# Pairing heads in the second mixer's attention: scores in the two row halves, values in the two column halves of the array

## The chip, the cores and the metric

The kernel runs on one core of a Trainium2 chip. The metric is the device time of one execution in microseconds: 2069.24 us is the median of three timed runs before the change (2062.05, 2069.24, 2071.39).

TensorE (PE) multiplies, PEld is its weight loader, VectorE is DVE, ScalarE is ACT, GpSimd is POOL, and SyncE (SP) issues the DMAs that carry weights from memory.

## What is computed

Two transformer blocks in a row on 256 tokens of width 1024, all in float32. Each block has a token mixer and then a mixture of experts. The change touches the attention of the second block's mixer alone:

```python
o_a = neighbourhood_attention(q_a * scale, k_a, v_a, k_ca, v_ca, rpb)   # 8 heads, each with its own keys
qb = axial_rope(rmsnorm(q_b, g_qn), row, col) * scale
kb = axial_rope(rmsnorm(k_b, g_kn), row, col)
k_all = concatenate([kb, k_cb]);  v_all = concatenate([v_b, v_cb])      # 256 tokens and 256 context rows
o_b = blocked_gqa(qb, k_all, v_all)                                     # 8 heads in 2 groups of 4
y = (sigmoid(g_a) * (o_a @ w_out_a) + sigmoid(g_b) * (o_b @ w_out_b)) @ w_o
```

A head has 64 dimensions. Each head attends from 256 queries to 256 tokens (in the neighbourhood attention with a bias and a window) and to 256 rows of context, so a softmax row has 512 entries. In the grouped attention heads 0 to 3 share the keys and values of group 0, heads 4 to 7 those of group 1. Behind the mixer the router picks 4 of 32 experts for each token, and the experts' weights follow.

## The kernel before

The kernel fixes the order of PE, DVE and ACT by hand: each of these engines runs its instructions in the order in which the source emits them. Weights come through a ring of 2 MB slots (`Ring`, from L98); SP issues the load of the next piece when a slot is given back, at L132.

The attention is a software pipeline over 32 steps (`Step`, from L2085, and the loop that ends at L2207). A step is one head and one half of the queries (128 rows). The first 16 steps are the neighbourhood heads, the last 16 the grouped heads. Head `h = 2b + s` in both halves; in the loop the query half `n` runs fastest, then `s`, then the pair number `b`. A step has these parts:

- `scores` (L2099): two products of 64 rows x 128 queries with 64 x 256 keys, tokens and context, into one of two `sc` buffers in PSUM. The queries and keys of a head lie in 64 of the 128 partitions, so a product uses one row half of the array (`tile_position=(p0, 0)`).
- `largest` (L2105 and L2106 grouped, L2109 to L2112 neighbourhood, DVE): the row maximum, with the bias added for the neighbourhood heads.
- `exps` (L2118, or L2120 and L2121, ACT): exponentials and their row sums into the tile `e`.
- `scaled` (L2126 to L2128, DVE): division by the sum.
- `turned` and `copied` (L2133 on PE, L2137 on ACT): four 128 x 128 transposes and a copy to `eT`, of which there are two buffers.
- `values` (L2145, PE): four products of 128 rows x 64 columns with `eT`, into 64 of the 128 partitions of the single tile `o` (one column half of the array). After the last step of a pair of heads ACT casts `o` out (L2148), and DVE makes the rest of the cast (`ended`, L2153).

An iteration emits the scores of step i, the values of step i - 2, the scaling of step i - 1, the maximum of step i, the exponentials of step i, and the transposes of step i - 1. Between them stand two calls `feed(2)`, which emit other projections (L703 on PE, with their casts L715 on ACT and L716 on DVE; each weight is split into a high and a low part), and three calls of `next(feed.behind)`, which sum condition vectors (L1949 ACT, L1951 POOL, L1952 and L1954 DVE, L479 PE) until they are done, late in the neighbourhood half. At step 16 `heads_to_columns` (L2166 to L2172) transposes the keys and queries of the grouped heads. A float32 product appears in the trace as two records.

The first mixer has a similar attention (loop at L1339). Its `values(pair)` (L1324) emits two heads in turn, each in its column half; its scores (L1280, L1281) are emitted one head at a time.

Behind the loop follow `w_out_a`, `w_out_b` and `w_o` (again L703), the router, and the second mixture of experts, whose weight loads (`w_gu`, `w_dn`) need the experts' order from the router and start with `ring.open()`.

Of the kernel before, what the change touches and what calls it, by code (L numbers as in the profile page):

```python
# [12 lines left out]
F32 = mybir.dt.float32  # L13
# [4 lines left out]
ALU = mybir.AluOpType  # L18
# [3 lines left out]
P = 128  # L22
D = 1024
T = 256
# [133 lines left out]
def _body(tc, nc, a, off, es, stop, dump):  # L158
    V, S, G, PE = nc.vector, nc.scalar, nc.gpsimd, nc.tensor
# [4 lines left out]
    def ps(tag, bufs, name=None):  # L164
        return psum.tile([P, 512], F32, tag=tag, bufs=bufs, name=name or tag)
# [77 lines left out]
    for q in range(8):  # L243
# [4 lines left out]
        for e in (4 * q, 4 * q + 2):  # L248
            pieces.append((("dn1", e), lambda t, e=e: load_dn1(t, e)))
    seq = [(key, piece_cols(win2, c0, n)) for key, c0, n in (("ka", 0, 512), ("qa", 1280, 512), ("kvb", 1024, 256), ("va", 512, 512),  # L250
           ("qb", 1792, 512), (("gab", 0), 2304, 512), (("gab", 1), 2816, 512), (("gab", 2), 3328, 512), (("gab", 3), 3840, 512))]
    for nm in ("w_out_a_2", "w_out_b_2"):
        seq.append((nm, lambda t, nm=nm: [(t.rearrange("p (c f) -> p c f", c=4), a[nm][0].rearrange("(c p) f -> p c f", p=P))]))
    for piece, conds in zip(seq, CONDS):
        pieces.append(piece)
        for i in conds:
# [726 lines left out]
    class Scan:  # L983
# [45 lines left out]
        def ended(self):  # L1029
            yb = yT[:, self.b]  # L1030
            V.scalar_tensor_tensor(yb, uT[:, self.b], dcol[:, self.b:self.b + 1], Scan.py[:, :T], op0=ALU.mult, op1=ALU.add)
            gelu(yb, yb, 5, yT[:, self.b + 1] if self.b < 3 else last_rot[:, 0, 0])
# [232 lines left out]
    class Look:  # L1265
# [10 lines left out]
        def scores(self):  # L1276
            self.pt = pt = ps("sc", 2)
            r = slice(64 * self.s, 64 * self.s + 64)
            q, kk = qT[r, self.blk], kz[r, self.br, self.gp]
            PE.matmul(pt[:, :P], q[:, :P], kk[:, :P], start=True, stop=True, tile_position=(64 * self.s, 0))  # L1280
            PE.matmul(pt[:, P:P + T], q[:, P:], kk, start=True, stop=True, tile_position=(64 * self.s, 0))  # L1281
# [803 lines left out]
    class Step:  # L2085
        def __init__(self, grouped, b, s, n):
            self.grouped, self.b, self.s, self.n = grouped, b, s, n
            self.h = 2 * b + s
            self.last = s == n == 1

        def scores(self):
            self.pt = pt = ps("sc", 2)
            if self.grouped:
                g, i = divmod(self.h, 4)
                p0, lq, keys = 64 * g, qbT[64 * g:64 * g + 64, i, :], (kbT, kbc)
            else:
                p0, lq, keys = 64 * self.s, qaT[64 * self.s:64 * self.s + 64, self.b, :], (kaT[:, self.b, :], kac[:, self.b, :])
            for i, kk in enumerate(keys):
                PE.matmul(pt[:, T * i:T * i + T], lq[:, P * self.n:P * self.n + P], kk[p0:p0 + 64], start=True, stop=True, tile_position=(p0, 0))  # L2099

        def largest(self):
            self.e = paw.tile([P, 512], F32, tag="e", bufs=3, name="e")
# [33 lines left out]
            self.eT = paw.tile([P, 512], F32, tag="eT", name="eT")  # L2136
            S.copy(self.eT, self.pt2)  # L2137

        def values(self):
            if (self.s, self.n) == (0, 0):  # L2140
                Step.po = ps("o", 1)
            out = Step.po[64 * self.s:64 * self.s + 64, P * self.n:P * self.n + P]
            v, vc, c0 = (vb, vbc, 64 * (self.h // 4)) if self.grouped else (va, vac, 64 * self.h)
            for j in range(4):
                PE.matmul(out, (v if j < 2 else vc)[:, j % 2, c0:c0 + 64], self.eT[:, P * j:P * j + P], start=(j == 0), stop=(j == 3),  # L2145
                          tile_position=(0, 64 * self.s))
            if self.last:
                S.copy(*self.ends(0))  # L2148

        def ended(self):  # L2150
            if self.last:
                hi, src = self.ends(0)
                V.tensor_tensor(self.ends(1)[0], src, hi.bitcast(F32), op=ALU.subtract)  # L2153

        def ends(self, i):

            dst, po = (obT if self.grouped else oaT)[i][:, self.b, :], Step.po[:, :T]
            if self.grouped:
                return dst, po
            return dst.rearrange("p (n t) -> p n t", n=2), backwards(po.rearrange("p (n t) -> p n t", n=2))  # L2160

    def heads_to_columns():

# [12 lines left out]
        V.tensor_scalar(x1[:, n], x1[:, n], rr[:, n, 3:4], None, op0=ALU.mult)  # L2176
    feed(64)
    feed.next = 1 << 30
    steps = [Step(grouped, b, s, n) for grouped in range(2) for b in range(4) for s in range(2) for n in range(2)]
    prev = last = None  # L2180
    for i, st in enumerate(steps + [None, None]):
        if i == 16:
            heads_to_columns()
            sg[1] = pk.tile([P, 4, T], F32, tag="sg2", name="sg2")
        if i == 18:
            obT.extend(pcx.tile([P, 4, T], F32R, tag=t, name="obT" + x) for t, x in (("kac", "h"), ("vac", "l")))
        if st:
            st.scores()
        if last:
            last.values()  # L2190
        if prev:
            prev.scaled()
        if st:
            st.largest()
        if last:
            last.ended()
        next(feed.behind, None)
        feed(2)
        if st:
            st.exps()  # L2200
        next(feed.behind, None)
        if prev:
            prev.turned()
            prev.copied()
        feed(2)
        next(feed.behind, None)
        prev, last = st, prev  # L2207
    if stop == "att2":
        nc.sync.dma_start(dump["oaT"], oaT[0].bitcast(F32))
        nc.sync.dma_start(dump["obT"], obT[0].bitcast(F32))  # L2210
# [631 lines left out]
```

## Time and profile before

| | before |
|---|---|
| median of 3 runs | 2069.24 us |
| profiled execution, its own time | 2064.46 us |
| its span | 2062.7 us |
| PE busy | 1801.3 us, 87% |
| DVE busy | 851.9 us, 41% |
| ACT busy | 547.0 us, 27% |
| DMA, mean | 306 GB/s |

The page cuts the span into 40 slices of 51.6 us; a digit is the busy share in tenths, and PEclk the granted clock of TensorE in tenths of full speed. The attention lies in slices 17 to 20 (counted from 1).

```profile
PE   5898998989898888999989689986799988999865
DVE  6998888453213237775554112221031211212112
PEclk7998899899999998799988989999899999999986
DMA  8634337866799976551346999999999999899996
```

A mean over the span mixes stages with different limits, so the change has to be read in the window of its own stage, and what follows has to be read for whether it starts earlier when the stage ends earlier.

### The profile page before, as it was taken

To read this page: it belongs to the slowest core of one execution; us is meant where nothing else is said; L and a number is where in the kernel's file an instruction comes from. 1 tells how busy PE (TensorE), PEld (TensorE's weight loads), DVE (VectorE), ACT (ScalarE), POOL (GpSimd) and SP (SyncE) were. 2 spreads that over 40 slices of the span, in tenths; PEclk is the share of its full clock that TensorE was granted. 3 is DMA by queue.
4 is the path that set the end of the run, shared out by engine and by line. 5 is a ranking of instruction groups with operands and counts; after the bars stand their busy time and mean duration, and the time that the engine had idled before them with its cause. 6 is when DMAs were issued, how large, how long until landed. Compare 5 with 4: busy or idle time off the path is not lost. (4 is left out here: it accounts for less than half of the span.)

```text
span 2062.7 us, 25525 instructions
## 1 busy us (share of the span) xinstructions
PE 1801.3 (87%) x10043; PEld 1015.8 (49%) x10043; DVE 851.9 (41%) x1832; ACT 547.0 (27%) x1184; POOL 258.7 (13%) x232
## 2 busy tenths in 40 slices
PE   5898998989898888999989689986799988999865
PEld 3677777876554437788964223332233333333211
DVE  6998888453213237775554112221031211212112
ACT  4443566232011125555432002110011111112001
POOL 2576322110000004430020000000000000000000
PEclk7998899899999998799988989999899999999986
DMA  8634337866799976551346999999999999899996
GB/s 259 229 113 163 111 107 228 276 246 248 287 364 397 393 282 200 194 184 59 128 166 269 423 416 424 420 423 423 417 419 419 424 420 420 340 421 419 423 422 256
DMA packets 172650, 630.82 MB, mean 306 GB/s; under 512 B 25408, under 2 KB 32000, under 8 KB 152032
## 3 DMA queue, kind: packets, MB, share of 16 engines
q1 hardware_dynamic: 172096, 628.04, 78.2%
q8 instruction: 89, 1.46, 0.3%
q10 hardware_dynamic: 288, 0.52, 0.1%
q0 software_dynamic: 128, 0.39, 0.1%
q14 instruction: 49, 0.40, 0.1%
HBM read 627.88 MB, written 1.05 MB: 305 GB/s over the span
## 5 line engine op out<-in xcount | busy, mean ns | idle before, releaser
L2543 PE MATMUL mm<-w,xT 128*64 128x512 f32 x1472 | 330.7, 603 | 0.0
L2543 PEld LDWEIGHTS mm<-w,xT 128*64 128x64 f32 x1472 | 103.2, 139 | 204.2 <-issue 198.6
L2634 PE MATMUL o<-w,aT 128*64 128x512 f32 x640 | 152.4, 612 | 3.2 <-DMA w<-in_w_dn 3.2
L2577 PE MATMUL mm<-w,xT 128*32 128x512 f32 x768 | 102.6, 663 | 39.1 <-DMA w<-in_w_gu 39.1
L2552 DVE TENSOR_SCALAR g<-mm 128x512 f32<-128x512 f32 x23 | 15.9, 692 | 261.2 <-PE mm L2543 261.2
L2811 POOL TENSOR_TENSOR fin<-acc,fin 128x512 f32<-128x512 f32 x1 | 1.3, 1275 | 975.4 <-DVE acc L2809 975.4
L716 DVE TENSOR_TENSOR lo<-w,hi 128x512 fp32r<-128x512 f32 x126 | 100.0, 806 | 30.4 <-ACT hi L715 28.4
L703 PE MATMUL mm<-hTh,scratch 128*128 128x256 f32 x392 | 98.0, 317 | 11.7 <-DVE scratch L716 11.7
L715 ACT CAST hi<-w 128x512 fp32r<-128x512 f32 x126 | 76.6, 618 | 63.7 <-PE mm L703 55.2
L2609 PE MATMUL o<-w,aT 128*32 128x512 f32 x384 | 70.8, 781 | 25.3 <-DMA w<-in_w_dn 23.3
L2634 PEld LDWEIGHTS o<-w,aT 128*64 128x64 f32 x640 | 45.4, 140 | 89.5 <-issue 81.8
L2554 ACT ACTIVATE s<-g 128x512 f32<-128x512 f32 x23 | 14.5, 632 | 274.5 <-DVE g L2552 274.4
L703 PEld LDWEIGHTS mm<-hTh,scratch 128*128 128x128 f32 x392 | 71.4, 203 | 29.9 <-issue 14.8
L1655 PE MATMUL mm<-w,xT 128*32 128x512 f32 x640 | 73.6, 605 | 7.2 <-DVEq L1841 2.7
L2649 DVE SCALAR_TENSOR_TENSOR yl<-yy,wc,yh 128x512 fp32r<-128x512 f32 (+1 forms) x30 | 21.4, 749 | 137.1 <-ACT yh L2648 136.9
L2577 PEld LDWEIGHTS mm<-w,xT 128*32 128x32 f32 x768 | 22.7, 114 | 105.4 <-DMA w<-in_w_gu 60.9
L703 PE MATMUL mm<-hT3h,lo 128*128 128x256 f32 x192 | 61.1, 318 | 9.0 <-DVE lo L716 6.4
L2639 ACT COPY yy<-o 64x512 f32<-64x512 f32 x40 | 23.2, 580 | 159.8 <-PE o L2634 159.5
L1630 PEld LDWEIGHTS sc<-Sm,x 128*128 128x128 f32 x256 | 61.7, 335 | 6.6 <-issue 5.0
L2664 DVE TENSOR_TENSOR acc<-acc,sc 128x512 f32<-128x512 f32 x56 | 37.0, 685 | 66.7 <-PE sc L2656 66.7
L1630 PE MATMUL sc<-Sm,x 128*128 128x128 f32 x256 | 63.2, 411 | 1.3 <-DVE Sm L1621 1.2
L703 PE MATMUL mm<-scratch 128*128 128x256 f32 x216 | 63.8, 295 | 0.0
(706 smaller groups left out, 3593.0 us busy)
## 6 DMA issues: line engine op xcount, KB each, us to landing
w<-in_w_gu SPq DMA_DIRECT2D x128, 2048.0 KB, 19.8
w<-in_w_dn SPq DMA_DIRECT2D x63, 2048.0 KB, 22.9
w<-in_w_in SPq DMA_DIRECT2D x20, 2048.0 KB, 10.5
w<-in_moe_w_gate SPq DMA_DIRECT2D x32, 1024.0 KB, 10.6
w<-in_moe_w_up SPq DMA_DIRECT2D x32, 1024.0 KB, 12.8
w<-in_moe_w_down SPq DMA_DIRECT2D x32, 1024.0 KB, 13.8
w<-in_ada_w SPq DMA_DIRECT2D x12, 2048.0 KB, 9.6
w<-in_w_mod SPq DMA_DIRECT2D x12, 2048.0 KB, 9.1
```

Source lines behind the costliest of these rows:

```text
L703: PE.matmul(out, x, y, start=start and i == 0, stop=stop and i == 2)
L715: S.copy(hi, src)
L716: return parts, lambda: V.tensor_tensor(lo, src, hi.bitcast(F32), op=ALU.subtract)
L1630: PE.matmul(pt[:, P * cc:P * cc + P], xv1[:, n, c, :], Sm[:, n].rearrange("p e s -> p (e s)"), start=(n == 0), stop=(n == 1))
L1655: PE.matmul(pg[32 * j:32 * j + 32, :].rearrange("p (j f) -> p j f", j=2), xT[:, c, 32 * j:32 * j + 32], w[:, c % 2], start=(c == 0), stop= ...
L2543: PE.matmul(pg[i][64 * j:64 * j + 64, :], bcast(ident[:, q:q + 1], [P, 64]) if c < 0 else xT[:, c, :], bgu if c < 0 else w[:, o:o + 512], ...
L2577: PE.matmul(pg[32 * t:32 * t + 32, :], xT[:, c, :], w[:, 512 * ij:512 * ij + 512], start=False, stop=(c == 7), tile_position=(0, 32 * t))
L2609: PE.matmul(pd[32 * t:32 * t + 32, :], aT[:, f % 4, 2 * (1 - e) + f // 4, :], w[:, 512 * j:512 * j + 512], start=False, stop=(f == 7), til ...
L2634: PE.matmul(pd[64 * j:64 * j + 64, :], aT[:, f % 4, f // 4, :], w[:, 512 * j:512 * j + 512], start=False, stop=(f == 7), tile_position=(0, ...
L2639: S.copy(y[:, 512 * j:512 * j + 512], pd[64 * j:64 * j + 64, :])
L2649: V.scalar_tensor_tensor(yl[:, o], y[:, o], back[1], yh[:, o].bitcast(F32), op0=ALU.mult, op1=ALU.subtract)
L2664: V.tensor_tensor(o, o, pc, op=ALU.add)
```

## The change

Two heads now go together, `s = 0` and `s = 1` of the same pair `b` and the same query half `n`; the loop's order is pair, query half, head. `scores(pair)` emits the four products of the two heads in turn, one in the row half 0 to 63 and one in the row half 64 to 127, each head into its own `sc` buffer. It is emitted for the next pair at the end of every odd iteration, and for the first pair ahead of the loop. `values(pair)` emits the eight products of two heads in turn, one in each column half, at every odd iteration for the steps i - 3 and i - 2. All else of a step stays one head at a time. The loop has 35 iterations instead of 34, and `heads_to_columns` stands in iteration 15 instead of 16.

So that two grouped heads lie in different row halves, the grouped pair `b` is now the heads `b` and `4 + b`, one of each group, instead of `2b` and `2b + 1`. The rows of `w_out_b` are loaded in the matching order, in two DMAs of 64 partitions each instead of one of 128.

```diff
-    for nm in ("w_out_a_2", "w_out_b_2"):
-        seq.append((nm, lambda t, nm=nm: [(t.rearrange("p (c f) -> p c f", c=4), a[nm][0].rearrange("(c p) f -> p c f", p=P))]))
+    seq.append(("w_out_a_2", lambda t: [(t.rearrange("p (c f) -> p c f", c=4), a["w_out_a_2"][0].rearrange("(c p) f -> p c f", p=P))]))
+    seq.append(("w_out_b_2", lambda t: [(t.rearrange("p (c f) -> p c f", c=4)[64 * g:64 * g + 64],
+                                         a["w_out_b_2"][0].rearrange("(g c d) f -> g d c f", g=2, c=4)[g]) for g in range(2)]))
...
-            self.h = 2 * b + s
-            self.last = s == n == 1
+            self.h = 4 * s + b if grouped else 2 * b + s
+            self.last = n == 1
+        def score(self, i):
+            if i == 0:
+                self.pt = ps("sc", 2)
+            r = slice(64 * self.s, 64 * self.s + 64)
+            q, keys = (qbT, (kbT, kbc)) if self.grouped else (qaT, (kaT[:, self.b, :], kac[:, self.b, :]))
+            PE.matmul(self.pt[:, T * i:T * i + T], q[r, self.b, P * self.n:P * self.n + P], keys[i][r], start=True, stop=True,
+                      tile_position=(64 * self.s, 0))
...
+    def scores(pair):
+        for i in range(2):
+            for st in pair:
+                st.score(i)
+    def values(pair):
+        if pair[0].n == 0:
+            Step.po = ps("o", 1)
+        for j in range(4):
+            for st in pair:
+                v, vc, c0 = (vb, vbc, 64 * st.s) if st.grouped else (va, vac, 64 * st.h)
+                PE.matmul(Step.po[64 * st.s:64 * st.s + 64, P * st.n:P * st.n + P], (v if j < 2 else vc)[:, j % 2, c0:c0 + 64],
+                          st.eT[:, P * j:P * j + P], start=(j == 0), stop=(j == 3), tile_position=(0, 64 * st.s))
+        if pair[0].last:
+            S.copy(*pair[0].ends(0))
...
-    steps = [Step(grouped, b, s, n) for grouped in range(2) for b in range(4) for s in range(2) for n in range(2)]
-    prev = last = None
-    for i, st in enumerate(steps + [None, None]):
-        if i == 16:
+    steps = [Step(grouped, b, s, n) for grouped in range(2) for b in range(4) for n in range(2) for s in range(2)]
+    scores(steps[0:2])
+    for i in range(35):
+        st = steps[i] if i < 32 else None
+        prev = steps[i - 1] if 0 < i < 33 else None
+        pair = steps[i - 3:i - 1] if i % 2 and i > 2 else None
+        if i == 15:
             heads_to_columns()
...
-        if st:
-            st.scores()
-        if last:
-            last.values()
+        if pair:
+            values(pair)
         if prev:
             prev.scaled()
         if st:
             st.largest()
...
         feed(2)
+        if i % 2 and i < 31:
+            scores(steps[i + 1:i + 3])
         next(feed.behind, None)
```

## Rows read from the trace of the kernel before

**Rows 1.** Windows: length, busy PE, PEld, DVE, ACT, POOL (instructions), PEclk, DMA, GB/s

```profile
928.67:990.67 62.00, 62.00 (x421) 51.54 (x422) 34.51 (x84) 31.98 (x68) 0.00 (x0) 1.00 0.20 71
1105.00:2040.00 935.00, 799.10 (x3916) 278.29 (x3912) 189.48 (x346) 129.35 (x257) 0.00 (x0) 0.94 0.99 411
```

**Rows 2.** Timeline of SP: start, length, queue, line, loads issued

```profile
923.45 0.38 SPq L132 DMA_DIRECT2D w<-in_w_out_b  x1
...
1088.67 9.66 SPq L132 DMA_DIRECT2D w<-in_w_gu  x3
```

**Rows 3.** Timeline of PE, one grouped step: start, length, line, out<-in, shapes, records

```profile
948.17 0.70 PE L2099 MATMUL sc<-kbT,qbT 64*128 64x256 f32 x2
...
949.22 0.65 PE L2145 MATMUL o<-eT,vb 128*64 128x128 f32 x4
...
950.24 0.39 PE L703 MATMUL mm<-hT3h,lo 128*128 128x256 f32 x1
...
951.07 0.60 PE L2133 MATMUL tr<-C,e 128*128 128x128 f32 x4
951.42 0.36 PE L703 MATMUL mm<-hT3h,lo 128*128 128x256 f32 x1
...
952.31 0.48 PE L2099 MATMUL sc<-kbT,qbT 64*128 64x256 f32 x1
```

**Rows 4.** Timeline of PE in a neighbourhood step at the lower clock

```profile
854.30 1.22 PE L2099 MATMUL sc<-kaT,qaT 64*128 64x256 f32 x2
...
856.31 1.11 PE L2145 MATMUL o<-eT,va 128*64 128x128 f32 x4
...
858.21 0.80 PE L703 MATMUL mm<-hi,hT3l 128*128 128x512 f32 x1
```

**Rows 5.** First mixer's values: timeline of PE, and L1324's window (PE, PEld)

```profile
270.10 0.87 PE L1324 MATMUL o<-eT,vt 128*64 128x256 f32 x8
...
270.10:270.80 0.70, 0.70 (x8) 0.56 (x10) 1.00 0.00 0
```

**Rows 6.** Timelines of DVE, ACT and PEld in grouped steps, idle before in brackets

```profile
953.47 0.69 DVE L2105 TENSOR_REDUCE mx<-sc 128x1 f32<-128x512 f32 x1 [0.58 <-PE sc L2099]
954.45 0.69 ACT L2118 ACTIVATE e<-sc,mx 128x512 f32<-128x512 f32 x1 [1.41 <-DVE mx L2106]
955.46 0.49 DVE L2128 TENSOR_SCALAR e<-e,su 128x512 f32<-128x512 f32 x1
955.88 0.59 ACT L2137 COPY eT<-tr 128x512 f32<-128x512 f32 x1 [0.66 <-PE tr L2133]
...
993.08 0.58 ACT L2137 COPY eT<-tr 128x512 f32<-128x512 f32 x1 [0.66 <-PE tr L2133]
993.72 0.41 PEld L2145 LDWEIGHTS o<-eT,vb 128*64 128x64 f32 x4 [0.23 <-ACT eT L2137]
```

**Rows 7.** Windows of the neighbourhood half, cut where the maximum of a step starts

```profile
836.98:857.70 20.72, 19.88 (x85) 14.89 (x86) 20.09 (x36) 11.84 (x27) 13.54 (x10) 0.64 0.66 231
857.70:871.51 13.81, 13.81 (x56) 9.72 (x55) 7.35 (x20) 5.02 (x13) 3.79 (x3) 0.67 0.42 150
871.51:883.11 11.60, 11.60 (x61) 8.45 (x62) 10.50 (x22) 7.44 (x18) 4.04 (x4) 0.89 0.67 235
883.11:889.15 6.04, 6.04 (x23) 4.52 (x23) 2.42 (x9) 2.70 (x7) 1.09 (x1) 0.65 1.04 382
889.15:920.66 31.51, 31.13 (x213) 26.02 (x214) 27.62 (x78) 19.09 (x51) 10.10 (x13) 1.00 0.30 108
920.66:928.67 8.01, 7.72 (x55) 6.47 (x56) 2.56 (x9) 3.72 (x11) 2.68 (x2) 1.00 0.51 175
```

**Rows 8.** Windows where PE pauses, in the neighbourhood half and in the first mixer

```profile
842.00:845.00 3.00, 2.16 (x9) 1.65 (x8) 2.96 (x7) 0.83 (x3) 2.26 (x2) 0.66 0.95 363
845.00:848.00 3.00, 3.00 (x8) 1.52 (x8) 2.96 (x4) 3.00 (x7) 2.56 (x2) 0.50 0.08 18
...
330.00:340.00 10.00, 9.23 (x73) 8.13 (x74) 9.66 (x28) 6.68 (x18) 4.93 (x3) 1.00 1.01 197
```

More of the change, by code (lines that the diff above doesn't have):

```diff
@@ L2087, in __init__ @@
             self.grouped, self.b, self.s, self.n = grouped, b, s, n
-            self.h = 2 * b + s
-            self.last = s == n == 1
[L2091 to L2099, printed above, removed]
+            self.h = 4 * s + b if grouped else 2 * b + s
[7 more added lines that the diff above has]
+                      tile_position=(64 * self.s, 0))
         def largest(self):
@@ L2137, in copied @@
             S.copy(self.eT, self.pt2)
[L2139 to L2153, printed above, removed]
         def ends(self, i):
@@ L2160, in ends, with ended @@
             return dst.rearrange("p (n t) -> p n t", n=2), backwards(po.rearrange("p (n t) -> p n t", n=2))
+    def scores(pair):
[12 more added lines that the diff above has]
+            S.copy(*pair[0].ends(0))
+    def ended(pair):
+        if pair[0].last:
+            hi, src = pair[0].ends(0)
+            V.tensor_tensor(pair[0].ends(1)[0], src, hi.bitcast(F32), op=ALU.subtract)
     def heads_to_columns():
@@ L2194, in _body @@
             st.largest()
-        if last:
-            last.ended()
+        if pair:
+            ended(pair)
         next(feed.behind, None)
@@ L2205, in _body @@
         feed(2)
+        if i % 2 and i < 31:
+            scores(steps[i + 1:i + 3])
         next(feed.behind, None)
-        prev, last = st, prev
     if stop == "att2":
```

## The prediction, made before the change was run

> **What bounds the kernel now.** I read the page's slices first, then windows by stretch, then the timeline of single steps. The chain of waits names only the last few microseconds, so the bound of the end is read from windows: from 1105 to 2040 us the DMA engines are 0.99 busy at 411 GB/s [rows 1]. That is the second MoE, streaming expert weights. The stream is let go only when the router has ordered the experts: after a long pause SP issues three loads of `w_gu` at 1088.67 [rows 2]. The router needs the mixer's output, so the attention (about 836 to 998 us) lies on the path to the start of the stream, and a microsecond less there moves everything behind it. PE, ACT and DVE run in the order of the source, so nothing else can fill a gap or be overtaken.
>
> Inside the attention I ask who is late. In the grouped half (step starts 928.67 to 990.67, 15 steps) PE is busy for all of 62.00 us and DVE for 34.51 [rows 1]: PE bounds it, at 62.00 / 15 = 4.13 us a step, 8.27 for two. One step is four pieces [rows 3]: scores 948.17 to 949.22, 1.05; values to 950.24, 1.02; projections to 951.07, transposes to 951.42 and projections to 952.31, 0.83 + 0.35 + 0.89 = 2.07. The sum is 4.14. In the neighbourhood half (836.98 to 928.67) it alternates: the first three steps keep DVE busy 20.09 of 20.72 us, while 857.70 to 871.51 leaves it idle for 6.46 [rows 7]. There PE is late, partly at the lower clock (granted 0.67).
>
> **Scores, two heads alternating in the row halves.** Nothing is added: 8 products of a pair are reordered. No row of before shows two row halves in turn, so the cost is bounded. Below: half of two heads' 2.10, so 1.05 for the pair; less is excluded, since each head's own products still take 1.05 in its half [rows 3]. Above: the halves take turns, 2.10; or each of the 8 changes costs a restart, at most the 0.23 for which the loader paused in a step [rows 6], 1.84 more, 3.94. I take 1.05, because the nearest rows, the column halves of the first mixer (below), do run side by side. The Trainium skill ("TensorE: Matmul & The Clock Gate", section "Measured speedup vs the span model") gives 3.07 times for four row tiles; by that efficiency two would give 1.53 times, a pair would take 1.37 by estimate, and 16 pairs would keep some 5 us more.
>
> **Values, two heads alternating in the column halves.** This arrangement is already in the first mixer, L1324: its first 8 records, for each head 2 of 256 and 2 of 128 columns, take 0.70 us, the loader busy 0.56 within it [rows 5]. That is 768 columns a head; a pair of the second mixer has 8 records of 128, 1024 columns: 0.70 x 1024 / 768 = 0.93 instead of 2.04. So the two packings free 1.05 + 1.11 = 2.16 us of PE per pair, 1.08 a step. At the lower clock scores take 2.01 and values 1.90 [rows 4], and about half of it goes, 1.95 a step.
> The Trainium skill (same page, "The mechanism") says that weight loads overlap running products only where the row groups differ, which would deny this gain, as both heads use all rows. The trace disagrees: 0.56 us of loads lie inside those 0.70 us [rows 5].
>
> **What the new order makes late.** Both score buffers now belong to one pair, so the next pair's scores wait for the second head's exponentials, and values of the last pair wait for an `eT` that was turned just before. I lay out a pair of the grouped half from the end of its scores, t = 0. PE does projections, transposes, projections until 2.07. DVE starts the maximum 0.11 after the scores (953.47 against 952.31 + 1.05), ACT's exponentials start 0.98 later, at 1.09 [rows 6]. ACT is free for the waiting `eT` copy about 0.7 later, the copy takes 0.59, and values start 0.06 behind a copy (993.66 to 993.72) [rows 6]: 2.42. So PE, ready at 2.07, stands 0.35. Values end at 3.35, the other 2.07 end at 5.42. Are the second head's exponentials done by then? Scaling of the first ends 1.50 after its exponentials began (954.45 to 955.95) [rows 6], at 2.59; the second's maximum takes 0.98 to the start of its exponentials, 3.57, later by 0.3 where the cast of the outputs stands before it in ACT's queue; 0.7 more is 4.6. That is 0.8 before 5.42, so the buffers cost nothing here. A pair takes 1.05 + 5.42 = 6.47; I take 6.6, as the casts for the projections share ACT's queue. **Grouped half: 8 x (8.27 - 6.6) = 13.4 us.** Without the stand it would be 8 x 2.16 = 17.3.
>
> **Neighbourhood half.** A stretch can gain no more than DVE's idle time in it, nor more than PE is relieved of [rows 7]. 836.98 to 857.70: idle 0.63, gain 0.6. 857.70 to 871.51, two steps at granted 0.67: idle 6.46, relief some 3.3, gain 3.3. 871.51 to 883.11: idle 1.10, gain 0.6. 883.11 to 889.15: idle 3.62, one step mostly at the lower clock, gain 1.7. 889.15 to 920.66, seven steps: idle 3.89, relief 7.6; each scaled pair needs a round of DVE, ACT and DVE, so I take 2.8. 920.66 to 928.67: idle 5.45, relief 1.1, gain 1.1 (the transposes of queries and keys move one step earlier here; they are the same ones, and projections now stand between them and the scores). **Sum 10.1.** Ends: 0 if every round trip is exposed, 16 if PE comes to the higher clock and 21 us of idle DVE shrink to 0.3 a step.
>
> **The rest, one answer each.** The grouped heads' pairing changes which rows of `obT` hold which head, and the load of `w_out_b` with it: two DMAs for one. The issue of one took 0.38 us at 923.45 [rows 2], SP has nothing due until the next slot is free, and the tile is used after all products of `w_out_a`. If that cover were gone, it would be 0.4 us. One more turn of the loop moves projections from behind it into it, at no cost. The first pair's scores stand together ahead of the loop: 1.05 us later for DVE at most, once. The outputs are cast after every second pair as before.
>
> **Sum.** 13.4 + 10.1 = 23.5 us. The profiled execution took 2064.46 us (span 2062.7), so it would be 2041.0. The three timed ones gave 2062.05, 2069.24 and 2071.39; the middle of the four is 2066.9, 2.4 below the median, and I forecast from it: 2043.
>
> **Rivals.**
> Row halves take turns: a pair costs 1.05 more, 7.65, the grouped half gains 5.0, the other about 5: 2057. For it: no row shows the halves together. Against: the column halves overlap.
> Column halves take turns, by the skill's rule above: 16 pairs lose 1.11, less what DVE hides, some 13 us: 2056. Against it stand the 0.70 us [rows 5].
> Buffers and round trips decide: where ACT's casts come between the two exponentials, PE waits out what packing freed, the grouped half stays at 8.27 and only 5 us of the other half remain: 2062. It decides if the second exponentials end later than 5.42; I found 4.6, with 0.8 to spare.
> More than forecast: no stand, and the higher clock in the first half, 17.3 + 16 = 33: 2034.
> Slower, by restarts: if each alternation of halves costs a restart, a pair has 7.52 + 8c for the restart c; at c = 0.09 the grouped half breaks even, at 0.23 it is 9.36, 8.7 us more there, and 0.55 a step in the eight or so steps of the other half that DVE doesn't bound, some 4: 2080.
> Slower, by the clock: PE now stands now and then, and at 842 to 845 it fell from busy (2.16 of 3.00) to a granted 0.50 in the next stretch, 1.2 GHz; in the first mixer it kept 1.00 with 9.23 of 10.00 busy [rows 8]. At 1.2 GHz scores and values took 1.9 times as long [rows 3, 4]; a pair's 6.12 of PE would be 11.6, so past a third of the grouped half at 1.2 its gain is gone, and all of it costs 8 x (11.6 - 8.27) = 27 us, less the 10 of the other half: 2084.
>
> **How the numbers follow.** Chances: forecast 0.60, row halves in turn 0.10, column halves 0.02, buffers 0.12, more 0.07, restarts 0.05, clock 0.04. The range runs from 2030 (below the rival with more by the spread of executions) to 2062, which leaves out half of the buffers' case, restarts and clock: 0.15. About 0.5%, 10 us, is what a measurement of this kernel can tell from no change. Faster by more: 0.77 (forecast, more, most of the turns); within: 0.15 (most of the buffers' case, some of turns and clock); slower: 0.08.
>
> **What would show it.** Step starts in the grouped half 6.5 apart for two, against 8.27; a pair's 8 score records in about 1.05 and its 16 value records in about 0.93; a stand of PE before values put down to the `eT` copy; SP's loads of `w_gu` after the router near 1065 instead of 1088.67, and the stream behind it as long as before. Scores of 2.1 or more would make the row step wrong, a stand before scores the buffers' step, and a granted clock of 0.50 in the grouped half the clock's.

## The result and the profile after

The changed kernel takes 2046.3 us, median of four executions (2040.22 to 2048.46), against 2069.2 for the kernel before: a ratio of 0.9893, 95% interval 0.9867 to 0.9919. The forecast was 2043 with a range of 2030 to 2062. The profiled execution is the fastest of the four, 2040.22 us with a span of 2038.5; the sum in the prediction gave 2041.0 for it.

The stretch that moved is the attention, as two landmarks show that every kernel below has: the first and the last start of the score products. First before, then after, in the view of one line's instructions (count, shortest/median/longest in ns, first and last start):

```profile
L2099 PE MATMUL sc<-kaT,qaT x32: 376/480/792, 835.8 to 919.8; 64*128 64x256 f32 x32
L2099 PE MATMUL sc<-kbT,qbT x32: 376/428/480, 927.5 to 989.8; 64*128 64x256 f32 x32
```

```profile
L2099 PE MATMUL sc<-kaT,qaT x32: 376/480/792, 834.8 to 905.0; 64*128 64x256 f32 x32
L2099 PE MATMUL sc<-kbT,qbT x32: 376/428/480, 915.3 to 964.6; 64*128 64x256 f32 x32
```

From the first scores to the last it was 989.8 - 835.8 = 154.0 us and is 129.8: 24.2 less, which is the whole difference of the two profiled executions (2064.46 - 2040.22 = 24.2). Up to the first grouped scores 91.7 became 80.5; from there to the last, 62.3 became 49.3. Part of this split comes only from the changed kernel emitting its scores a pair ahead. Counted from one step's maximum to another's, as in the prediction, the neighbourhood half went from 91.7 to 83.8 (the windows below), and the 15 grouped steps that took 62.00 before [rows 1] take 48.0 (first and last start of L2106: 919.8 and 967.8).

Behind the attention everything only moved. SP's queue issues the expert weights at 1063.94 instead of 1088.67 [rows 2], and the second MoE streams them as before [rows 1]; the timeline of SP's queue, then the windows (length, busy us of PE, PEld, DVE, ACT and POOL, granted clock, DMA share, GB/s):

```profile
1063.94 16.66 SPq L132 DMA_DIRECT2D w<-in_w_gu  x5
```

```profile
836.01:919.77 83.76, 73.35 (x494) 57.62 (x492) 73.34 (x173) 48.92 (x125) 35.62 (x31) 0.90 0.57 193
...
882.28:906.40 24.12, 21.11 (x173) 17.55 (x174) 22.22 (x66) 14.92 (x43) 7.18 (x11) 1.00 0.25 88
906.40:913.82 7.42, 6.86 (x61) 5.88 (x59) 7.32 (x13) 5.07 (x12) 5.36 (x4) 1.00 0.64 257
919.77:974.56 54.79, 54.20 (x472) 46.71 (x473) 36.85 (x90) 33.98 (x75) 0.41 (x1) 1.00 0.33 98
1081.00:2016.00 935.00, 796.90 (x3918) 277.90 (x3918) 189.50 (x346) 129.33 (x257) 0.00 (x0) 0.95 0.99 411
```

From the issue to the end of the span it is 974.56 us, before 974.03. In the grouped half PE is still busy throughout, 54.20 of 54.79: it bounds the half as before, with less to do. In the neighbourhood half DVE is now busy 73.34 of 83.76 us, and 29.54 (22.22 + 7.32) of the 31.54 from 882.28 to 913.82.

One pair of the grouped half, PE's timeline (start, length, record, count; compare [rows 3]) and, below it, ACT's:

```profile
931.65 0.70 PE L2099 MATMUL sc<-kbT,qbT 64*128 64x256 f32 x4
932.19 0.60 PE L2099 MATMUL sc<-kvbc,qbT 64*128 64x256 f32 x4
932.72 0.39 PE L705 MATMUL mm<-hT3h,lo 128*128 128x256 f32 x1
...
934.77 0.87 PE L2160 MATMUL o<-eT,vb 128*64 128x128 f32 x7
...
936.11 0.38 PE L705 MATMUL mm<-hT3h,lo 128*128 128x256 f32 x1
...
938.16 0.70 PE L2099 MATMUL sc<-kbT,qbT 64*128 64x256 f32 x4
```

```profile
934.47 0.58 ACT L2138 COPY eT<-tr 128x512 f32<-128x512 f32 x1
936.22 0.37 ACT L2163 CAST obTh<-o 128x256 fp32r<-128x256 f32 x1 [1.18 <-PE o L2160]
936.49 0.63 ACT L717 CAST hi<-w 128x512 fp32r<-128x512 f32 x1
937.01 0.69 ACT L2119 ACTIVATE e<-sc,mx 128x512 f32<-128x512 f32 x1
```

Four score records of two heads now lie in the 0.70 us in which two of one head lay before. A pair's scores take 931.65 to 932.72, 1.07 us; its values 934.77 to 936.11, 1.34; the pair comes round in 938.16 - 931.65 = 6.51, against 8.27.

### The profile page after: what moved, and what is told of

Same layout as the page of the kernel before. It is cut to its first block, busy times and chain, and to the rows that moved or that the text cites. A ratio compares the mean times of both kernels' runs of the same rounds, so it can differ in the third digit from the quotient of the medians.

```text
span 2038.5 us, 25531 instructions
## 1 busy us (share of the span) xinstructions
PE 1767.2 (87%) x10043; PEld 990.5 (49%) x10043; DVE 854.2 (42%) x1832; ACT 544.2 (27%) x1184; POOL 258.6 (13%) x232
## 3 DMA queue, kind: packets, MB, share of 16 engines
HBM read 627.88 MB, written 1.05 MB: 309 GB/s over the span
## 5 line engine op out<-in xcount | busy, mean ns | idle before, releaser
L2619 PE MATMUL o<-w,aT 128*32 128x512 f32 x384 | 69.1, 752 | 25.7 <-DMA w<-in_w_dn 23.9
L705 PEld LDWEIGHTS mm<-hTh,scratch 128*128 128x128 f32 x392 | 71.7, 204 | 28.1 <-issue 14.1
```

Of the source, the lines that this page charges most:

```text
L705: PE.matmul(out, x, y, start=start and i == 0, stop=stop and i == 2)
L2619: PE.matmul(pd[32 * t:32 * t + 32, :], aT[:, f % 4, 2 * (1 - e) + f // 4, :], w[:, 512 * j:512 * j + 512], start=False, stop=(f == 7), til ...
```

## The experiments

The times, with the ratio to the kernel before on the same chip, and the lengths by the landmarks above in the profiled execution (us):

| kernel | time | ratio (95%) | first to last scores | neighbourhood | grouped |
|---|---|---|---|---|---|
| before | 2069.2 | | 154.0 | 91.7 | 62.3 |
| after | 2046.3 | 0.9893 (0.9867 to 0.9919) | 129.8 | 80.5 | 49.3 |
| after, again | 2046.1 | 0.9894 (0.9875 to 0.9913) | 131.7 | 82.3 | 49.4 |
| values in turn | 2047.4 | 0.9892 (0.9874 to 0.9910) | 134.1 | 83.2 | 50.9 |
| scores in turn | 2040.7 | 0.9865 (0.9846 to 0.9884) | 129.8 | 80.4 | 49.4 |
| both in turn | 2047.4 | 0.9894 (0.9878 to 0.9911) | 133.3 | 83.0 | 50.3 |
| whole array between | 2077.2 | 1.0040 (1.0020 to 1.0061) | 162.1 | 93.3 | 68.8 |
| values later | 2037.0 | 0.9832 (0.9809 to 0.9854) | 126.7 | 80.4 | 46.3 |
| scores earlier | 2045.5 | 0.9881 (0.9854 to 0.9909) | 134.6 | 82.1 | 52.5 |
| GpSimd additions left out | 7763.8, once, with another routing | | 122.8 | 73.7 | 49.1 |
| GpSimd additions doubled | 2061.3, once | | 143.9 | 94.0 | 49.9 |
| values later, scores in turn | 2037.7 | 0.9858 (0.9834 to 0.9882) | 125.6 | 79.2 | 46.4 |
| values later, two turns | 2038.5 | 0.9865 (0.9840 to 0.9891) | 126.1 | 78.9 | 47.2 |
| values later, one turn | 2031.3 | 0.9814 (0.9792 to 0.9836) | 120.1 | 69.1 | 51.0 |

The first scores start between 828.5 and 839.7 in these executions, although nothing ahead of them was edited: 11 us that no edit here explains. The lengths come from one profiled execution of each kernel, whose own time can lie well off the median beside it (2031.35 against 2037.7 for values later, scores in turn), and the runs were made on several chips, each beside the kernel before on its own. So the columns on the right carry the verdicts, and differences of the time column under some 5 us are read with care.

**The yardstick.**

> The changed kernel itself once more, as the yardstick for the runs beside it on the same chip. Expected from its first profile: two steps of the grouped half 6.52 us apart, a pair's eight score records over 1.07, values to the next projections 1.34, the neighbourhood half 83.8 us long, and the same 20 to 25 us under the kernel before.

129.8 and 131.7 us from first to last scores: 2 us of difference between two executions of one kernel, nearly all in the neighbourhood half. The grouped half repeats to 0.1.

**Is it the alternation?** Theory: two heads' products run side by side in the two halves of the array. Rival: the halves take turns, and the gain lies in the new order of the steps. The obvious test is to take the alternation back, for the values, the scores, and both.

```
-        for j in range(4):
-            for st in pair:
+        for st in pair:
+            for j in range(4):
                 v, vc, c0 = ...
```

> Only the value products go head by head again (8 in the first column half, then 8... i.e. 4 of the first head, then 4 of the second), the scores stay alternating. My theory (column halves run side by side): a pair's values need 2 x 1.02 = 2.04 us as in the kernel before; the stand for the second eT copy disappears in the first head's 1.02, so values to projections go from 1.34 to 2.04, two steps from 6.52 to 7.22, the grouped half is 8 x 0.70 = 5.6 us longer, the neighbourhood half 1 to 4 us, in all 6 to 10 us slower than the changed kernel. Rival (column halves take turns anyway, by the rule of the Trainium skill, page TensorE: Matmul & The Clock Gate, section The mechanism, that weight loads overlap only between different row groups): the order makes no difference, 0 us.

```
-        for i in range(2):
-            for st in pair:
+        for st in pair:
+            for i in range(2):
                 st.score(i)
```

> Only the score products go head by head again, the values stay alternating. My theory (row halves run side by side): a pair's four products take 2.10 us instead of 1.07. The first head's maximum can start 1.05 before the end of the pair's scores, so the stand for the eT copy before values (about 0.35) may go: two steps from 6.52 to 7.2 to 7.6, the grouped half 5.5 to 8.4 us longer, the neighbourhood half 2 to 4, in all 8 to 12 us slower than the changed kernel. Rival (row halves take turns, the gain came from elsewhere): 0 us.

> Both kinds of products go head by head, in the new order of pairs with its new buffers. My theory (all of the gain is the packing): PE needs 2.10 + 2.04 + 4.14 = 8.28 us for two steps, the grouped half is back at 66 us (before: 8.27 for two), the neighbourhood half near its 91.7 of before, and the time within 5 us of the kernel before. Rival (the gain comes from the order: paired steps, projections between scores and values): most of the 23 us stay although nothing runs side by side.

All three missed. With scores in turn the grouped half is 49.4, as with alternation; with values in turn it grows by 1.5 and not by 5.6; with both, 1.0. Read alone, that is the rival's result. The timeline of PE in the run with both in turn says otherwise; in its program the order is all of the first head, then all of the second:

```profile
937.21 0.65 PE L2160 MATMUL o<-eT,vb 128*64 128x128 f32 x4
937.70 0.27 PE L2160 MATMUL o<-eT,kvbc 128*64 128x128 f32 x1
937.70 0.32 PE L2160 MATMUL o<-eT,vb 128*64 128x128 f32 x1
...
938.72 0.39 PE L705 MATMUL mm<-hT3h,lo 128*128 128x256 f32 x1
...
940.79 0.71 PE L2099 MATMUL sc<-kbT,qbT 64*128 64x256 f32 x4
941.32 0.61 PE L2099 MATMUL sc<-kvbc,qbT 64*128 64x256 f32 x4
941.86 0.39 PE L705 MATMUL mm<-hT3h,lo 128*128 128x256 f32 x1
```

The four `kbT` records, two of each head, all start ahead of the four `kvbc`, which begin 0.53 us after the first of them, although the first head's `kvbc` products stand before the second head's `kbT` in the program. So PE took the second head's products up beside the first head's: 1.07 us for the pair. Of the values, where a head has eight records and not four, the second head's first record (`vb` at 937.70) starts together with the first head's fifth (`kvbc` at 937.70): half of the work overlaps, 938.72 - 937.21 = 1.51 us for the pair, where 2.04 would be none. A late `eT` copy of the second head is not the reason: for the pair at 914.14 of the same run the copy had ended at 911.45 + 0.59 = 912.04, 2.1 us ahead, and the second head (`va` at 914.63) still starts beside the first one's fifth record (`vac` at 914.62).

The edit had not taken the packing away. And what was taken for granted ahead of the prediction and in it, that PE runs in the order of the source and nothing there can be overtaken, does not hold between two halves of the array.
The Trainium skill ("TensorE: Matmul & The Clock Gate", section "The mechanism") says that products start and end strictly in program order. These rows differ: products of another half started ahead of three earlier records, both in the scores and in the values.

**Parting the halves.** To part the two heads, a product that needs the whole array was put between them, with both orders in turn as above:

```
                 self.pt = ps("sc", 2)
+                if self.s:
+                    PE.matmul(self.pt[:, :32], ident, ident[:, :32], start=True, stop=True)
...
+            if st.s:
+                PE.matmul(Step.po[:, 256:288], ident, ident[:, :32], start=True, stop=True)
             for j in range(4):
```

> Head by head as in the run with both in turn, and between the two heads' scores, and between their values, one small added product over the whole array (the identity by 32 of its columns, into columns that are overwritten or never read), 64 of them. Theory (the halves run side by side whenever the two heads' products stand next to each other, in whatever order; a product that needs the whole array parts them): scores 2.1 plus 0.1 to 0.3 us for the added one, values 2.04 plus 0.1 to 0.3, two steps 8.4 to 8.8 us instead of 6.52, the grouped half 15 to 18 us longer and the other 6 to 10, so about the time of the kernel before, 2065 to 2075. Rival (the gain comes from pairs and the order of the steps, not from halves side by side): two steps rise only by the added products, to 6.7 to 7.1, and the time stays under 2053.

```profile
939.56 0.70 PE L2101 MATMUL sc<-kbT,qbT 64*128 64x256 f32 x2
940.10 0.59 PE L2101 MATMUL sc<-kvbc,qbT 64*128 64x256 f32 x2
940.62 0.41 PE L2098 MATMUL sc<-C 128*128 128x32 f32 x2
940.96 0.70 PE L2101 MATMUL sc<-kbT,qbT 64*128 64x256 f32 x2
941.49 0.59 PE L2101 MATMUL sc<-kvbc,qbT 64*128 64x256 f32 x2
942.01 0.39 PE L705 MATMUL mm<-hT3h,lo 128*128 128x256 f32 x1
...
948.51 0.70 PE L2101 MATMUL sc<-kbT,qbT 64*128 64x256 f32 x2
```

Now the heads stand one behind the other: 1.06 + 0.34 for the added product + 1.05. A pair takes 948.51 - 939.56 = 8.95 us. Without its two added products of 0.34 (the one in the values, L2161, starts at 945.10, the products behind it at 945.44) that is 8.27, which is the pair of the kernel before to the hundredth. So the new order of the steps brings nothing in the grouped half, the packing brings all of it, and the rival falls there. In the neighbourhood half the sum can't be made so cleanly: it takes 93.3 us against 80.5, but with 16 added products, some of them hidden where DVE is late, so how much of its gain is packing is not shown. The whole kernel is slower than before, 2077 us, a little past what was expected; the 32 added products, 10.9 us at 0.34 each by estimate, are enough to account for it.

**The stand before values.** (A stand is time in which PE waits in place.) In the changed kernel the first head's values start at 934.77, but the second head's `eT` copy runs until 934.47 + 0.58 = 935.05, and the pair takes 1.34. Two edits move work in between. First, values behind two projections:

```
-        if pair:
-            values(pair)
         if prev:
             prev.scaled()
         if st:
             st.largest()
-        if pair:
-            ended(pair)
         next(feed.behind, None)
         feed(2)
+        if pair:
+            values(pair)
         if st:
             st.exps()
+        if pair:
+            cast(pair)
+            ended(pair)
```

> The values of a pair stand after the first two projections of the step instead of before them, and the cast of the outputs after the exponentials. Theory (PE stands 0.35 us a pair for the second head's eT copy): the stand goes, two steps take 6.17 instead of 6.52, the grouped half is 2.5 us shorter and the neighbourhood half 0 to 3, the time 2 to 5 us under the changed kernel. Rival (the later cast and the later values push the next buffers): the second exponentials end later than the next scores begin, PE stands before scores instead, 0 or up to 3 us slower.

```profile
935.85 0.66 PE L2160 MATMUL o<-eT,vb 128*64 128x128 f32 x8
...
936.88 0.65 PE L2134 MATMUL tr<-C,e 128*128 128x128 f32 x4
...
938.17 0.70 PE L2099 MATMUL sc<-kbT,qbT 64*128 64x256 f32 x4
...
944.33 0.70 PE L2099 MATMUL sc<-kbT,qbT 64*128 64x256 f32 x4
```

All eight `vb` records in one go, the pair's values 936.88 - 935.85 = 1.03, and two steps in 944.33 - 938.17 = 6.16 as expected: the stand cost 0.31 to 0.35 a pair. The grouped half is 3.0 us shorter, first to last scores 3.1 to 5.0. The median fell by 9, more than that, the profiled executions only by 1.1 and 4.3 (2039.13 against 2040.22 and 2043.47); what the median lost beyond the attention's 3 to 5 stays unexplained.

Second, the next scores ahead of the last two projections:

```
-        feed(2)
         if i % 2 and i < 31:
             scores(steps[i + 1:i + 3])
+        feed(2)
```

> The next pair's scores stand ahead of the second two projections of the odd step instead of behind them, so 0.89 us earlier on PE, and the projections then cover the round trip to the values. Theory of the prediction (the second exponentials are done 0.8 us before the scores; the trace of the changed kernel shows 0.45): PE stands 0.4 us before scores, the stand of 0.35 before values goes, two steps stay at 6.5 to 6.6: -1 to +2 us against the changed kernel. If buffers don't bind: two steps at 6.17 and 3 us faster. If the exponentials are late by more: two steps above 6.9 and 3 us slower or more.

```profile
936.70 1.11 PE L2160 MATMUL o<-eT,vb 128*64 128x128 f32 x7
...
939.65 0.85 PE L2099 MATMUL sc<-kbT,qbT 64*128 64x256 f32 x3
...
941.08 0.39 PE L705 MATMUL mm<-hT3h,lo 128*128 128x256 f32 x1
...
943.84 0.74 PE L2160 MATMUL o<-eT,vb 128*64 128x128 f32 x8
```

The buffers bind: this pair's scores take 941.08 - 939.65 = 1.43 instead of 1.07, since the second head's first record starts only at 940.34, after the exponentials that free its buffer (939.19 to 939.88), and values to values is 7.14. The grouped half grew by 3.2 us, which is the third of the cases named, by more than the 0.4 that the theory allowed. The time does not show it, 2045.5 against 2046.1 and 2046.3; it is read from the attention alone. The stand before values stayed in the first of these two pairs (the `vb` records at 936.70 take 1.11), where ACT's second `eT` copy ran until 937.22; in the next pair it ended at 943.87, 0.03 behind the start of the values. In this attention, whoever moves the scores forward pays with the buffers; whoever moves the values back does not.

**The order of scores on top.**

> Values later as in the run before, and the scores head by head. Theory (order within a pair's scores is immaterial, the 5 us that the run with scores in turn had less lay outside the attention): from the first to the last scores 126 to 128 us as with values later alone, two steps 6.16, and the time 2034 to 2040. Rival (scores in turn let the first maximum start earlier and are worth 5 us by themselves): 122 us from first to last scores, the time near 2032.

125.6 us against 126.7, and 2037.7 against 2037.0: the order of a pair's scores is immaterial here too. The run with scores in turn alone had a median 5 us under the changed kernel's at the same 129.8 from first to last scores (the profiled executions differ by 1.1); that difference did not come again and lies outside the attention.

**What held back the neighbourhood half?** The forecast gain of 2.8 us in its last long stretch did not come. Two DVE instructions in the changed kernel's timeline stand out, and what GpSimd did then:

```profile
909.47 1.66 DVE L1954 SCALAR_TENSOR_TENSOR w<-w,cs 128x512 f32<-128x512 f32 x1
911.05 1.22 DVE L2127 TENSOR_TENSOR su<-su 128x1 f32<-128x1 f32 x1
```

```profile
909.26 3.00 POOL L1953 TENSOR_TENSOR w<-w 128x512 f32<-128x512 f32 x2 [1.63 <-ACT w L1951]
912.34 1.28 POOL L1958 TENSOR_TENSOR part<-w 128x512 f32<-128x512 f32 x1
```

The sum of two columns takes 1.22 us and the scaled addition 1.66, where the one at 908.70, nearly all of it ahead of GpSimd's start, takes 0.74. Theory: DVE's instructions are lengthened by GpSimd's additions beside them. One run leaves the additions of L1953 out (those of L1958 stay), another makes each of them twice.

```
-                        G.tensor_tensor(w[:, 0], w[:, 0], w[:, c], op=ALU.add)
```

> Leaves out the GpSimd additions of the even chunks in the conditions' column sums (the sums lack those chunks, so the routing behind may differ and only the attention's stretch is read). Theory (DVE's instructions are lengthened while GpSimd adds beside them, which took the forecast gain of the second part of the neighbourhood half): the sum of two partial sums takes 0.15 us at every step instead of up to 1.22, the scaling 0.49 instead of up to 1.39, DVE is busy 6 to 10 us less in the neighbourhood half, which gets 4 to 8 us shorter. Rival (DVE's instructions were long for another reason): the same lengths as before and the half shorter by under 1 us.

```
                         G.tensor_tensor(w[:, 0], w[:, 0], w[:, c], op=ALU.add)
+                        G.tensor_tensor(s, w[:, 0], w[:, c], op=ALU.add)
```

> The changed kernel, with each of GpSimd's 24 additions of the conditions in this stage made a second time into a tile that is overwritten later; nothing on DVE, PE or ACT is added. Theory (DVE's instructions are lengthened while GpSimd adds beside them): DVE is busy 5 to 12 us more in the neighbourhood half without one more instruction, the scaled additions of the conditions go from 957 ns towards 1100 or more, and the half gets 3 to 10 us longer. Rival (GpSimd's additions only cost when somebody waits for their result): DVE's instructions keep their lengths, the half gets 0 to 3 us longer by waits for GpSimd.

The groups of DVE by line in the neighbourhood half (count, busy us, mean ns of one, idle before), first after, then without the additions, then with each twice (a window with two scaled additions more); line numbers differ by one:

```profile
L1954 DVE SCALAR_TENSOR_TENSOR w<-w,cs 128x512 f32<-128x512 f32 x15 | 14.4, 957 | 0.1
L2127 DVE TENSOR_TENSOR su<-su 128x1 f32<-128x1 f32 x16 | 7.1, 444 | 1.0 <-ACT e L2122 1.0
L2112 DVE TENSOR_REDUCE mx<-sc 128x1 f32<-128x256 f32 x16 | 6.7, 417 | 0.0
```

```profile
L1953 DVE SCALAR_TENSOR_TENSOR w<-w,cs 128x512 f32<-128x512 f32 x15 | 11.2, 747 | 0.1
L2126 DVE TENSOR_TENSOR su<-su 128x1 f32<-128x1 f32 x15 | 3.4, 224 | 1.1 <-ACT e L2121 1.1
```

```profile
L1955 DVE SCALAR_TENSOR_TENSOR w<-w,cs 128x512 f32<-128x512 f32 x17 | 22.2, 1304 | 0.1
L2128 DVE TENSOR_TENSOR su<-su 128x1 f32<-128x1 f32 x15 | 9.2, 616 | 0.9 <-ACT e L2123 0.9
L2113 DVE TENSOR_REDUCE mx<-sc 128x1 f32<-128x256 f32 x16 | 6.7, 417 | 0.0
```

Mean 747, 957 and 1304 ns for the scaled addition, 224, 444 and 616 for the sum of two columns, with none, one and two of L1953's additions in each place; in the second execution of the changed kernel it was 1073 and 464. The maximum over the scores, which DVE reads from PSUM, stays at 417. Without the additions DVE is busy 62.63 us in the half (168 instructions) instead of 72.68 (170); GpSimd is still busy 13.76, so some lengthening is left. The neighbourhood half takes 73.7, 80.5 to 82.3, and 94.0 us. The theory stands, and by more than was expected of the doubled additions (3 to 10 us). With these PE's granted clock was also lower in the half, 0.77 against 0.90, but DVE was busy 87.84 of its 94.00 us. Without the additions, only the attention's stretch is read: the routing behind is another one there.
The Trainium skill ("SBUF — State Buffer", section "Who interferes with whom") says that a DVE instruction with two inputs in SBUF contends with a GpSimd instruction that reads SBUF, and that a reduction never does. These rows agree, with 747 to 1304 ns for the one and 417 for the other; but the maximum reads PSUM, so they do not test a reduction that reads SBUF.

**A use of that.** In the grouped half PE is late and DVE is not, so the conditions' work is better done there. Their generator gets three turns a step; fewer turns spread it. The edit, on top of values later, takes away the last of the three `next(feed.behind, None)` in the loop:

> Values later, and the conditions get two turns per step instead of three, so a third of their work moves from the neighbourhood half, where DVE is late, to the grouped half, where PE is. Theory: the neighbourhood half loses a third of the conditions' DVE time (some 22 us with their lengthening) and part of the lengthening of the rest, 4 to 7 us shorter; the grouped half stays at two steps in 6.2, as PE bounds it; the time 2030 to 2034. Rival (weights for the projections, which share the ring of slots with the conditions' weights, arrive later): PE waits for projections, 0 or slower.

A miss: GpSimd's last addition ahead of a pause began at 875.4 instead of 873.9, then all stood until 903.7 (901.7 without this edit) for the next weights. The turns taken away were turns without work, and neither the half (78.9) nor the time (2038.5) moved beyond the spread. With one turn a step:

> Values later, and the conditions get one turn per step. With two turns nothing left the neighbourhood half: GpSimd's additions ended at 875.4 instead of 873.9, and then all stood still until 903 for the next condition's weights, so the turns taken away were turns without work. Theory: with one turn (36 are needed, the loop has 35) the additions spread over the empty stretch from 875 to 903 and into the grouped half; the DVE time and the lengthening move under PE's bound there, the neighbourhood half falls from 80 to 72 to 76 us, the grouped half stays within 1 us of 46.4 and the time is 2030 to 2035. Rival (the slots of the ring come free later, so the projections' weights come later, or the conditions left at the end of the loop are waited for behind it): PE waits for weights or the tail behind the scores, 99 to 100 us, gets longer by what the half gains, 2037 or more.

The neighbourhood half fell to 69.1, 11 us under values later alone, more than expected. Of the 15 additions of L1953 only 3 moved to the grouped half. The others are spread over the neighbourhood half, and the division by the sum is no longer lengthened; its 15 instructions took, in values later and then here:

```profile
L2129 DVE TENSOR_SCALAR e<-e,su 128x512 f32<-128x512 f32 x15 | 12.4, 828 | 0.5
```

```profile
L2129 DVE TENSOR_SCALAR e<-e,su 128x512 f32<-128x512 f32 x15 | 7.3, 489 | 0.5
```

DVE's busy time in the half fell from 72.20 to 63.42 us, 5.1 of it in this line and 3.0 in the three scaled additions that left (14.4 to 11.4); the other lines nearly cancel. The grouped half grew by 4.7, which was not: PE is busy for nearly all of it (50.73 of 51.00), has 16 more of the conditions' small products there, 2.1 us, and its granted clock was 0.84 and 0.85 from 911.20 to 921.20 and to 931.20, so part of the time the lower of its two levels (1.2 and 2.4 GHz), after 9.73 busy us of the 10.00 before; the changed kernel had 1.00 in this half. First to last scores is 120.1, and the kernel takes 2031.3 us (2028.7 to 2035.0), ratio 0.9814 with an interval of 0.9792 to 0.9836: the lowest median of those run, 15 us under the changed kernel. The interval overlaps that of values later (0.9809 to 0.9854).

## Why the prediction was right, point by point

- **The path.** That the stream starts when the attention lets it, and is as long as before, was right: issue at 1063.94, forecast near 1065, and 974.56 us behind it.
- **Scores.** 1.05 was taken between bounds of 1.05 and 3.94; 1.07 measured. No restart on a change of halves shows in it. The 1.37 estimated from the Trainium skill ("TensorE: Matmul & The Clock Gate", section "Measured speedup vs the span model") did not come either.
- **Values.** 0.93 by the first mixer's record; 1.03 measured where nothing waits (values later). The stand before them was forecast at 0.35 and is 0.31 by 1.34 - 1.03. It lies inside the pair's values and not ahead of them: the first head's products start, and the second's wait.
- **The grouped pair.** Laid out at 6.47, taken as 6.6 for casts in ACT's queue, measured 6.51. The 0.13 was caution that nothing paid for; the half gained 8 x (8.27 - 6.51) = 14.1 by this pair instead of 13.4, and 14.0 (62.0 to 48.0) from its first maximum to its last.
- **The buffers.** The second exponentials were forecast done 4.6 after the pair's scores, 0.8 to spare. They end at 937.70, 4.98 after 932.72, with 0.46 to spare, because a cast for the projections (936.49) stands before them on top of the outputs' cast. The conclusion held, the spare was half of what was stated, and scores earlier showed what lies behind it.
- **The neighbourhood half.** By the prediction's own windows 91.69 became 83.76: 7.9 gained for 10.1 forecast. The mis-sized term is the stretch of seven steps, forecast at 2.8: 31.54 us against 31.51, no gain. Its working took DVE's busy time of 27.62 as fixed [rows 7]. It rose to 29.54, because more of DVE's work now falls beside GpSimd's additions, and DVE's time depends on that. That GpSimd lengthens DVE's work is shown by the two runs. That the change brought more of it together here is read from the windows: GpSimd was busy 10.10 us in this stretch and 2.68 in the step behind it, where DVE has time to spare [rows 7]; now it is 12.54 (7.18 + 5.36) and 0.00. This makes 1.9 of the missing 2.8; the rest is DVE's idle time, forecast to fall from 3.89 to 1.1 and measured at 2.00. The other stretches missed by less and nearly cancel: the first three steps gained nothing for 0.6, the next two 3.5 for 3.3, the two after them nothing for 0.6, the eighth step 2.6 for 1.7, the last 2.1 for 1.1.
- **The rivals.** Row halves in turn and column halves in turn fell with the 1.07 and the 1.03; the clock was 1.00 in the grouped half. Of the working behind them one assumption was wrong without touching the sum: that alternation is what makes the halves run together. It is enough that the two heads' products stand next to each other.
- **The sum.** Its closeness is in part luck. Of the 24.2 us the neighbourhood half gave 7.9 for 10.1 and the grouped steps 14.0; 1.9 came behind the last maximum (98.0 to 96.1 up to the issue) and 1.0 from an earlier start that no edit explains, less 0.5 in the stream. The 2.2 that were missing were made up there.

The median came out 3 us above the 2043 and the profiled execution 1 us below its 2041; both lie within the spread of the executions (2040.2 to 2050.4 for the changed kernel on two occasions).

## What to carry to other kernels

Put products that fit in different halves of the array next to each other in the program, and keep products over the whole array from between them; the fine order within matters little with four records a head (1.07 us in either order) and more with eight (1.51 against 1.03). When packing shortens PE's work, look next for the copy that the packed products wait for, and put other products over it, rather than moving the producers' own scores forward into full buffers. And before a busy engine's time is taken as fixed in a sum, see what runs beside it: DVE's time here was 10 us longer by GpSimd's additions, and spreading these so that fewer fell beside DVE's long instructions took 6.6 us off the attention (126.7 to 120.1), where the last polish of the order on PE, values later, took 3.1 to 5.0.

## What the runs showed of the hardware that was not expected

- PE started products of one half of the array ahead of earlier products of the other half, in the rows here ahead of three of them: a pair's scores took 1.07 us in either order, its values 1.51 head by head and 1.03 alternating. One added product over the whole array, 0.34 us, ended this: 2.45 us for the scores.
- DVE's scaled additions from SBUF took 747, 957 to 1073, and 1304 ns with none, one and two GpSimd additions in each place; the maximum, which reads PSUM, kept 417 ns. The division by the sum, one input from SBUF, took 0.49 us away from GpSimd's additions and 1.39 beside one (912.51, beside 912.34).
